# The opening of a decoder layer on one core: a modulation sum ahead of the last diagonal, the shift in two parts, other orders of requests and passes

## The chip, the cores and the metric

The kernel runs on one core of a Trainium2 chip. The metric is device time in microseconds (us) of one execution on that core. The core's engines are called as in the profile: PE is TensorE (matrix products), PEld its weight loads, DVE is VectorE, ACT is ScalarE, POOL is GpSimd, and SP is SyncE, which here only issues transfers. ACT issues transfers too; a letter q behind an engine's name marks its queue of issues.

## The reference

One layer of a hybrid decoder, in float32, for 512 tokens of width 1024. Only its beginning matters here: the modulation of the condition `c`, the first norm, and the first products.

```python
cond = jax.nn.silu(c)
mod = cond @ ada_w[l] + ada_b[l]
sh1, sc1, g1, sh2, sc2, g2 = jnp.split(mod[:, None, :], N_MOD, axis=-1)

u = rms_norm(x, mix_pre_g[l]) * (1.0 + sc1) + sh1
proj = u @ w_in[l]
qk_raw, v, o_pre, gates, glu = jnp.split(
    proj, [2 * D_ML, 3 * D_ML, 4 * D_ML, 4 * D_ML + 2 * H], axis=-1)
...
a, gt = jnp.split(glu, 2, axis=-1)
y = causal_dwconv(a * jax.nn.sigmoid(gt), cv_dw_w[l], cv_dw_b[l])
...
```

`rms_norm` divides each token by the root of its mean square and multiplies by a gain. Behind these lines follow the mLSTM heads, the convolution group, the output projection, and a feed-forward part with a convolution; all of that is the same in both kernels.

## The kernel before, in words

**Layout.** The width of 1024 is cut into 8 blocks of 128 (index k or j), the 512 tokens into 4 tiles of 128 (index tt). `u` is kept with channels on the partitions: u[k] is a block of 128 channels by 512 tokens. Products are made in three terms: every operand z is split into a high part (rounded to the type that TensorE takes, written by ACT) and a low part (z minus the high part, by DVE or POOL). A product is then high by high, high by low and low by high (`mm3`, lines 186 to 190), all added up in one PSUM bank.

**The opening** is what the change touches: lines 118 to 369, run in the first 56 us. It does two things at once. It makes u[0] to u[7], and it makes the first eight output tiles of the gated group (`glu`, banks0, one PSUM bank each), with k as the outer loop: as soon as u[k] and the block of weights for k (`wglu0_k`) are there, its products are added to all eight banks.

- `c` comes as two rows of 512 (`crow`); TensorE spreads them over all partitions (`cps`, line 139) and ACT makes `cb` = silu of that (line 253).
- `x` comes in eight pieces `xn[tt][hf]` of 256 KB, half the width each; the first halves are asked for on SP, the second halves on ACT. For each tile the squares are summed (ACT line 250 for the one half, DVE line 251 for the other), added (`xs`, DVE line 259) and raised to the power -1/2 on POOL (line 260).
- `x_turn` (line 237) multiplies an identity matrix by that factor (`dg`, DVE line 240). With dg as the moving operand TensorE turns blocks 0 to 3 of the tile into `xT_ps` (four banks) with the norm's factor applied (line 242), and with a matrix of ones it makes `rb_ps`, the factor spread over the partitions (line 243). Blocks 4 to 7 come from memory already turned (`xr`, line 328) and use `rb`.
- The modulation of block k is two sums over 1024 products each, `ada` times `cb`, on DVE (`ada_sum`, line 271): one for the scale, one for the shift, into the two columns of `part[k]`. `gsk` holds the gain `gs` (line 331: scale plus 1 plus bias, times the norm's gain; `bp1` and `g32` are small prepared vectors) and the shift `sh` (line 332).
- u[0] high is made by ACT from xT_ps[0] with gs and sh (line 336); DVE makes the exact value xr[0] (line 337) and the low part (line 338). ACT copies the other three banks of xT_ps out (line 286), as TensorE needs the banks for glu.
- `passes` (line 313) issues the 24 products of one k: the pairs (weight high, u high), (weight low, u high), (weight high, u low), each over the banks given. For k=0 it is called for banks 4 to 7 with all three pairs, then for banks 0 to 3. For k of 1 to 3 it is called once over all eight; from k=4 `mm3` is used bank by bank.

**What sets the order.** For SP and TensorE the order of the program text is kept. On DVE, ACT and POOL a scheduler places instructions by a model of their times. The context `opening` (`in_order`, lines 70 to 82) chains all instructions of those three engines that are written inside it, so that they keep the order of the text among themselves; an instruction written elsewhere may still be placed between them. Two of these are lines 398 and 444: `cvw` and `ghalf`, small vectors scaled by 0.5 for the convolution and the head norm, taken from `vec`, whose later columns are asked for at k=1 (line 325).

**Buffers.** `raws` has two buffers of 1 MB for ada, `adas` two of 512 KB for wglu0; a new block is asked for when the one two before has been used. The requests of one k on SP are: wglu0 block k (line 321), ada of block k+1 in two halves (line 225), at k=1 the rest of vec, for k of 1 to 4 one block of xr.

## Time and profile before

| what | value |
|---|---|
| time, three runs | 774.97 us median (774.62 to 776.15) |
| the profiled execution | 774.97 us, of which the span from first to last instruction is 773.2 |
| TensorE busy | 759.2 us, 98% of the span |
| DVE, ACT, POOL busy | 602.0, 399.8 and 350.9 us |
| transferred | 125.33 MB, mean 162 GB/s |

The profile is of one execution. Its timeline rows give the start in us from the span's start, the duration in us, the engine, the line of the kernel, the operation, the tiles it writes and reads, its shape and the count of instructions merged into the row; in brackets stands how long the engine had been idle before it and what ended that. Tile numbers are left out, so that wglu_1h is the high part of the second half of any wglu0 block. Ends of matrix products are modelled, and some of their records are missing.

### The profile page before, as it was taken

Reading aid. Unit: us, or ns where it says so; the run is one execution under the profiler, and the core shown is the slowest. Engines: PE = TensorE matmul, PEld = TensorE weight load, DVE = VectorE, ACT = ScalarE, POOL = GpSimd, SP = SyncE. Lnnn points to the kernel's source line nnn. Section 1 sums busy time; section 2 is a strip of 40 time slices with the busy share of each in tenths; the row PEclk is TensorE's granted clock in tenths of the full one; section 3 lists DMA queues with packets and bytes.
Section 4 is the critical chain, followed back from the end, with each engine's and each line's share of the span. In section 5 each row is a group of like instructions: output and inputs, shape, how many; then the busy total and the mean of one; then the engine's idle time right before and its main releaser. Section 6 shows DMA issues by size and latency. Waiting matters only on the chain.

```text
span 773.2 us, 10567 instructions
## 1 busy us (share of the span) xinstructions
PE 759.2 (98%) x3691; PEld 635.8 (82%) x3691; DVE 602.0 (78%) x955; ACT 399.8 (52%) x753; POOL 350.9 (45%) x286
## 2 busy tenths in 40 slices
PE   7999999999999999999999999999999999999996
PEld 5778898778888888888888998888888888888885
DVE  6977999999999864446858798666555687699996
ACT  5437266687676446472243545444444444455752
POOL 2029677697798644443661456444444440000001
PEclk9999999999999999999999999999999999999998
DMA  9984214204123452434953653332233321777872
GB/s 331 352 309 140 84 55 164 82 29 145 47 81 110 164 169 104 164 108 162 385 183 117 256 193 136 130 129 92 106 117 129 130 90 61 270 269 222 301 260 109
DMA packets 36409, 125.33 MB, mean 162 GB/s; under 512 B 4194, under 2 KB 5634, under 8 KB 30468
## 3 DMA queue, kind: packets, MB, share of 16 engines
q1 hardware_dynamic: 24372, 96.17, 35.4%
q10 hardware_dynamic: 11984, 28.48, 10.6%
q8 instruction: 29, 0.48, 0.2%
q14 instruction: 24, 0.20, 0.1%
HBM read 113.22 MB, written 11.42 MB: 161 GB/s over the span
## 4 chain that ended last, share of the span: by engine, by line
PE 82%; DVE 8%; DMA 5%; ACT 2%; issue 2%; POOL 0%; ACTq 0%; SPq 0%; DVEq 0%; POOLq 0%
PE up L189 10%; PE up L190 10%; PE up L188 10%; PE qko L188 5%; PE qko L189 4%; PE qko L190 4%; PE p L190 3%; PE p L189 3%; PE p L188 3%; PE o L496 2%; PE glu L189 2%; PE glu L190 2%; PE glu L188 2%; DMA wglu<-in_w_glu 2%; PE s L485 2%
## 5 line engine op out<-in xcount | busy, mean ns | idle before, releaser
L694 DVE SCALAR_TENSOR_TENSOR cv<-gt,cvw,cv 128x489 f32<-128x489 f32 (+23 forms) x200 | 136.9, 729 | 2.6 <-ACT cv L682 1.5
L648 POOL TENSOR_TENSOR ro2r<-ro2t,mhalf 128x1 f32<-128x1 f32 x1 | 0.5, 539 | 120.6 <-DVE ro2t L646 120.6
L171 POOL TENSOR_TENSOR wup_1024l<-wup,wup_1024h 128x512 fp32r<-128x512 f32 x20 | 27.8, 1390 | 31.3 <-ACT wup_1024h L170 21.9
L690 POOL TENSOR_TENSOR cs<-cs,cs 128x510 f32<-128x510 f32 (+3 forms) x32 | 41.2, 1289 | 0.2
L171 POOL TENSOR_TENSOR wup_0l<-wup,wup_0h 128x512 fp32r<-128x512 f32 x20 | 27.3, 1367 | 29.4 <-ACT wup_0h L170 29.4
L171 POOL TENSOR_TENSOR wup_1536l<-wup,wup_1536h 128x512 fp32r<-128x512 f32 x20 | 28.1, 1403 | 27.5 <-ACT wup_1536h L170 27.5
L155 DVE SCALAR_TENSOR_TENSOR junk<-ada,cb 128x1024 bf16<-128x1024 f32 x20 | 32.4, 1619 | 7.3 <-DMA ada<-in_adaT 7.1
L189 PE MATMUL up<-u2l,wup_0h 128*128 128x512 f32 (+1 forms) x100 | 36.5, 365 | 0.2 <-DVE u2l L870 0.2
L188 PE MATMUL up<-u2h,wup_0h 128*128 128x512 f32 (+1 forms) x100 | 36.5, 365 | 0.0
L188 PE MATMUL up<-u2h,wup_1024h 128*128 128x512 f32 (+1 forms) x100 | 36.4, 364 | 0.0
L190 PE MATMUL up<-u2h,wup_0l 128*128 128x512 f32 (+1 forms) x100 | 36.4, 364 | 0.0
L188 PE MATMUL up<-u2h,wup_512h 128*128 128x512 f32 (+1 forms) x100 | 36.4, 364 | 0.0
L189 PE MATMUL up<-u2l,wup_512h 128*128 128x512 f32 (+1 forms) x100 | 36.4, 364 | 0.0
L188 PE MATMUL up<-u2h,wup_1536h 128*128 128x512 f32 (+1 forms) x100 | 36.4, 364 | 0.0
L189 PE MATMUL up<-u2l,wup_1536h 128*128 128x512 f32 (+1 forms) x100 | 36.4, 364 | 0.0
L190 PE MATMUL up<-u2h,wup_512l 128*128 128x512 f32 (+1 forms) x100 | 36.4, 364 | 0.0
L190 PE MATMUL up<-u2h,wup_1536l 128*128 128x512 f32 (+1 forms) x100 | 36.4, 364 | 0.0
L190 PE MATMUL up<-u2h,wup_1024l 128*128 128x512 f32 (+1 forms) x100 | 36.4, 364 | 0.0
L189 PE MATMUL up<-u2l,wup_1024h 128*128 128x512 f32 (+1 forms) x100 | 36.3, 363 | 0.0
L171 POOL TENSOR_TENSOR wup_512l<-wup,wup_512h 128x512 fp32r<-128x512 f32 x20 | 27.7, 1384 | 14.8 <-ACT wup_512h L170 14.8
L688 ACT ACTIVATE cs<-gt,cvw 128x511 f32<-128x511 f32 (+4 forms) x40 | 27.4, 715 | 9.5 <-POOL cs L690 4.5
L170 ACT ACTIVATE wup_1024h<-wup 128x512 fp32r<-128x512 f32 x22 | 13.9, 630 | 24.7 <-PE up L189 20.1
(1046 smaller groups left out, 2641.6 us busy)
## 6 DMA issues: line engine op xcount, KB each, us to landing
wup<-in_w_up SPq DMA_DIRECT2D x22, 1024.0 KB, 6.8
wqko<-in_w_qko SPq DMA_DIRECT2D x12, 1024.0 KB, 4.8
ada<-in_adaT ACTq DMA_DIRECT2D x20, 512.0 KB, 4.7
ada<-in_adaT SPq DMA_DIRECT2D x16, 512.0 KB, 6.9
wo<-in_w_out SPq DMA_DIRECT2D x8, 1024.0 KB, 4.8
spare<-in_adaT ACTq DMA_DIRECT2D x12, 512.0 KB, 7.2
wd<-in_w_down SPq DMA_DIRECT2D x6, 768.0 KB, 5.9
g2kept<-g2d SPq DMA_DIRECT2D x11, 384.0 KB, 7.3
```

Of the source, the lines that this page charges most:

```text
L155: t = V.scalar_tensor_tensor(out=junk, in0=r, scalar=1.0, in1=cb, op0=ALU.mult, op1=ALU.mult, accum_out=mod[:, i : i + 1])
L170: S.activation(hi[:, :n], src, AF.Copy)
L171: (eng or G).tensor_tensor(out=lo[:, :n], in0=src, in1=hi[:, :n].bitcast(F32), op=ALU.subtract)
L188: PE.matmul(ps, a[0], b[0], start=start, stop=False)
L189: PE.matmul(ps, a[0], b[1], start=False, stop=False)
L190: PE.matmul(ps, a[1], b[0], start=False, stop=stop)
L485: PE.matmul(sp[:, :n], ks[d][:, cc * P : (cc + 1) * P], qs[d][:, cc * P :], start=d == 0, stop=d == 1)
L496: PE.matmul(o[:, : DH + 2], E[h][cc][:, a : a + P], vs[h][cc], start=cc == 0, stop=cc == tt)
L648: G.tensor_tensor(out=r, in0=t, in1=mhalf[:, :1], op=ALU.pow)
L688: S.activation(t[:, d:], cvx[j][:, : T - d], AF.Copy, scale=w(CK - 1 - d))
L690: G.tensor_tensor(out=side[:, d:], in0=side[:, d:], in1=t[:, d:], op=ALU.add)
L694: last_tap[0] = V.scalar_tensor_tensor(out=cp[:, d:], in0=cvx[j][:, : T - d], scalar=w(CK - 1 - d), in1=cp[:, d:], op0=ALU.mult, op1=ALU.add)
```

## The change

Six edits, all in or around the opening.

1. Requests: on SP, x's first piece is asked for ahead of `c`; `c` and the first columns of `vec` (before: on ACT) follow it, then x's other first halves. The shift half of ada's block 0 is asked for in two pieces of 256 KB.
2. In `x_turn` the rb product is issued ahead of the four xT products.
3. `bp1` and `g32` are made ahead of the loop over x's tiles instead of behind the sums.
4. The scale sum of block 0 stands on DVE ahead of the last tile's `x_turn`. The shift sum of block 0 is made in two halves of 512; the gain is computed between them, the bias is added to the first half's result, and the second half's is added to that.
5. At k=0: xr[0] is made by ACT instead of DVE, the two sums for block 1 stand on DVE between the weight splits and ahead of u[0] low, and the products go in the order: banks 4 to 7 with u high, banks 0 to 3 with u high, then all eight banks with u low.
6. `cvw` and `ghalf` are chained behind the last DVE instruction of the loop.

```diff
@@ -118,13 +118,15 @@
     vec = const.tile([P, NVEC], F32, name="vec")
     cb = const.tile([P, D], F32, name="cb")
     crow = slots.tile([P, T], F32, tag="t", name="crow"), slots.tile([P, T], F32, tag="t", name="crow")
-    for hf in range(2):
-        nc.sync.dma_start(crow[hf][:1, :], c[hf * T : (hf + 1) * T].rearrange("(a n) -> a n", a=1))
     xn = [[slot(f"xn{tt}_{hf}") for hf in range(2)] for tt in range(NT)]
+    FIRST = VEC["mix_pre_g"][1]
     for tt in range(NT):
         for hf in range(2):
             (nc.scalar if hf else nc.sync).dma_start(xn[tt][hf], x[tt * P : (tt + 1) * P, hf * T : (hf + 1) * T])
-    FIRST = VEC["mix_pre_g"][1]
+        if tt == 0:
+            for hf in range(2):
+                nc.sync.dma_start(crow[hf][:1, :], c[hf * T : (hf + 1) * T].rearrange("(a n) -> a n", a=1))
+            nc.sync.dma_start(vec[:, :FIRST], vecs[:, :FIRST])
 
     def vcol(name, i):
         a = VEC[name][0] + i
@@ -221,12 +223,11 @@
     def first_load(k):
 
         r = raws.tile([P, 2048], F32, tag="raw", name=f"ada{k}")
-        for i in range(2):
-            nc.sync.dma_start(r[:, i * D : (i + 1) * D], adaT[k][:, i * D : (i + 1) * D])
+        for a, b in ((0, D), (D, 2 * D)) if k else ((0, D), (D, D + T), (D + T, 2 * D)):
+            nc.sync.dma_start(r[:, a:b], adaT[k][:, a:b])
         first.append(r)
 
     first_load(0)
-    nc.scalar.dma_start(vec[:, :FIRST], vecs[:, :FIRST])
 
     opening = in_order()
     opening.__enter__()
@@ -238,9 +239,23 @@
 
         dg = slot(f"dg{tt}")[:, :P]
         V.tensor_scalar(out=dg, in0=ident, scalar1=xs[:, 1:], scalar2=None, op0=ALU.mult)
+        PE.matmul(rb_ps[:, tt * P : (tt + 1) * P], ones, dg, start=True, stop=True)
         for j in range(TURNED):
             PE.matmul(xT_ps[j][:, tt * P : (tt + 1) * P], xn[tt][j // NT][:, j % NT * P : (j % NT + 1) * P], dg, start=True, stop=True)
-        PE.matmul(rb_ps[:, tt * P : (tt + 1) * P], ones, dg, start=True, stop=True)
+
+    bp1 = const.tile([P, KT], F32, name="bp1")
+    V.tensor_scalar(out=bp1, in0=vcols("ada_b", 0, 2 * KT).rearrange("p (j two) -> p j two", two=2)[:, :, 0], scalar1=1.0, scalar2=None,
+                    op0=ALU.add)
+    g32 = const.tile([P, KT], F32, name="g32")
+    V.tensor_scalar(out=g32, in0=vcols("mix_pre_g", 0, KT), scalar1=RD, scalar2=None, op0=ALU.mult)
+    part = {}
+
+    def ada_sum(k, i):
+        if i == 0:
+            part[k] = small.tile([P, 2], F32, tag="adap", name=f"adap{k}")
+        junk = small.tile([P, D], BF16, tag="junk", bufs=1, name=f"junk{k}_{i}")
+        V.scalar_tensor_tensor(out=junk, in0=first[k][:, i * D : (i + 1) * D], scalar=1.0, in1=cb, op0=ALU.mult, op1=ALU.mult,
+                               accum_out=part[k][:, i : i + 1])
 
     xT_ps = [mmbank(f"xT{j}") for j in range(TURNED)]
     rb_ps = atbank("rb")
@@ -258,28 +273,23 @@
         last = small.tile([P, 2], F32, tag="gsk", name=f"xs{tt}")
         V.tensor_scalar(out=last[:, :1], in0=xsq[:, :1], scalar1=xsq[:, 1:], scalar2=D * EPS, op0=ALU.add, op1=ALU.add)
         G.tensor_tensor(out=last[:, 1:], in0=last[:, :1], in1=mhalf[:, :1], op=ALU.pow)
+    ada_sum(0, 0)
     x_turn(NT - 1, last)
     rb = slot("rb_s")
     S.activation(rb, rb_ps, AF.Copy)
 
-    part = {}
-
-    def ada_sum(k, i):
-        if i == 0:
-            part[k] = small.tile([P, 2], F32, tag="adap", name=f"adap{k}")
-        junk = small.tile([P, D], BF16, tag="junk", bufs=1, name=f"junk{k}_{i}")
-        V.scalar_tensor_tensor(out=junk, in0=first[k][:, i * D : (i + 1) * D], scalar=1.0, in1=cb, op0=ALU.mult, op1=ALU.mult,
-                               accum_out=part[k][:, i : i + 1])
-
-    for i in range(2):
-        ada_sum(0, i)
-
-    bp1 = const.tile([P, KT], F32, name="bp1")
-    V.tensor_scalar(out=bp1, in0=vcols("ada_b", 0, 2 * KT).rearrange("p (j two) -> p j two", two=2)[:, :, 0], scalar1=1.0, scalar2=None,
-                    op0=ALU.add)
-    g32 = const.tile([P, KT], F32, name="g32")
-    V.tensor_scalar(out=g32, in0=vcols("mix_pre_g", 0, KT), scalar1=RD, scalar2=None, op0=ALU.mult)
     xr = [slot(f"xr{j}") for j in range(KT)]
+
+    gsk0 = small.tile([P, 2], F32, tag="gsk", name="gsk0")
+    for a in (D, D + T):
+        junk = small.tile([P, D], BF16, tag="junk", bufs=1, name=f"junk0_{a}")
+        V.scalar_tensor_tensor(out=junk[:, :T], in0=first[0][:, a : a + T], scalar=1.0, in1=cb[:, a - D : a - D + T], op0=ALU.mult,
+                               op1=ALU.mult, accum_out=part[0][:, 1:])
+        if a == D:
+            V.tensor_scalar(out=gsk0[:, :1], in0=part[0][:, :1], scalar1=bp1[:, :1], scalar2=g32[:, :1], op0=ALU.add, op1=ALU.mult)
+            V.tensor_scalar(out=part[0][:, :1], in0=part[0][:, 1:], scalar1=vcol("ada_b", 1), scalar2=None, op0=ALU.add)
+        else:
+            V.tensor_tensor(out=gsk0[:, 1:], in0=part[0][:, 1:], in1=part[0][:, :1], op=ALU.add)
 
     def x_out(j, eng):
         if eng is S:
@@ -310,8 +320,8 @@
 
     banks0 = [mmbank(f"glu{i}") if i < 4 else atbank(f"glu{i}") if i < 6 else cvbank(f"glu{i}") for i in range(G0)]
 
-    def passes(wk, k, which):
-        for a, b in ((0, 0), (1, 0), (0, 1)):
+    def passes(wk, k, which, sides=((0, 0), (1, 0), (0, 1))):
+        for a, b in sides:
             for i in which:
                 PE.matmul(banks0[i], blk(wk, i)[a], u[k][b], start=k == 0 and a == b, stop=False)
 
@@ -326,23 +336,25 @@
         if 1 <= k <= TURNED:
             j = TURNED + k - 1
             nc.sync.dma_start(xr[j], xT[j - TURNED])
-        gsk = small.tile([P, 2], F32, tag="gsk", name=f"gsk{k}")
+        gsk = small.tile([P, 2], F32, tag="gsk", name=f"gsk{k}") if k else gsk0
         gs, sh = gsk[:, :1], gsk[:, 1:]
-        V.tensor_scalar(out=gs, in0=part[k][:, :1], scalar1=bp1[:, k : k + 1], scalar2=g32[:, k : k + 1], op0=ALU.add, op1=ALU.mult)
-        V.tensor_scalar(out=sh, in0=part[k][:, 1:], scalar1=vcol("ada_b", 2 * k + 1), scalar2=None, op0=ALU.add)
+        if k:
+            V.tensor_scalar(out=gs, in0=part[k][:, :1], scalar1=bp1[:, k : k + 1], scalar2=g32[:, k : k + 1], op0=ALU.add, op1=ALU.mult)
+            V.tensor_scalar(out=sh, in0=part[k][:, 1:], scalar1=vcol("ada_b", 2 * k + 1), scalar2=None, op0=ALU.add)
         hi, lo = u[k]
         if k == 0:
             wk[1] = w_split(r[:, T:], "wglu0_0_1", eng=V)
             S.activation(hi, xT_ps[0], AF.Identity, scale=gs, bias=sh)
-            V.tensor_scalar(out=xr[0], in0=xT_ps[0], scalar1=gs, scalar2=sh, op0=ALU.mult, op1=ALU.add)
+            ada_sum(1, 0)
+            wk[0] = w_split(r[:, :T], "wglu0_0_0", eng=V)
+            S.activation(xr[0], xT_ps[0], AF.Identity, scale=gs, bias=sh)
+            ada_sum(1, 1)
             V.tensor_tensor(out=lo, in0=xr[0], in1=hi.bitcast(F32), op=ALU.subtract)
-            wk[0] = w_split(r[:, :T], "wglu0_0_0", eng=V)
             for j in range(1, TURNED):
                 x_out(j, S)
-            for i in range(2):
-                ada_sum(1, i)
-            passes(wk, k, range(4, G0))
-            passes(wk, k, range(4))
+            for which in (range(4, G0), range(4)):
+                passes(wk, k, which, ((0, 0), (1, 0)))
+            passes(wk, k, range(G0), ((0, 1),))
             continue
         if k >= TURNED:
             V.scalar_tensor_tensor(out=xr[k], in0=xr[k], scalar=gs, in1=rb, op0=ALU.mult, op1=ALU.mult)
@@ -358,7 +370,7 @@
         if k < TURNED:
             V.tensor_tensor(out=lo, in0=xr[k], in1=hi.bitcast(F32), op=ALU.subtract)
         else:
-            V.scalar_tensor_tensor(out=lo, in0=xr[k], scalar=sh, in1=hi.bitcast(F32), op0=ALU.add, op1=ALU.subtract)
+            last_u = V.scalar_tensor_tensor(out=lo, in0=xr[k], scalar=sh, in1=hi.bitcast(F32), op0=ALU.add, op1=ALU.subtract)
         if k + 1 < KT:
             ada_sum(k + 1, 1)
         if k < 4:
@@ -370,6 +382,10 @@
     for i, ps in enumerate(banks0):
         glu_ps[i // 2, i % 2] = ps
 
+    def behind_opening(op):
+        tc.add_manual_dep(op.ins, last_u.ins.name, mybir.DependencyInfo(mybir.DependencyClass.NoSync, mybir.DependencyReason.DATA),
+                          reason="order on VectorE")
+
     cvx = [None] * KT
 
     def glu_gate(i):
@@ -395,7 +411,7 @@
         glu_gate(i)
 
     cvw = const.tile([P, CK * KT], F32, name="cvw")
-    V.tensor_scalar(out=cvw, in0=vcols("cv_dw_w", 0, CK * KT), scalar1=0.5, scalar2=None, op0=ALU.mult)
+    behind_opening(V.tensor_scalar(out=cvw, in0=vcols("cv_dw_w", 0, CK * KT), scalar1=0.5, scalar2=None, op0=ALU.mult))
 
 
     vs = [None] * H
@@ -441,7 +457,7 @@
         return t
 
     ghalf = const.tile([P, KT], F32, name="ghalf")
-    V.tensor_scalar(out=ghalf, in0=vcols("ml_norm_g", 0, KT), scalar1=0.5, scalar2=None, op0=ALU.mult)
+    behind_opening(V.tensor_scalar(out=ghalf, in0=vcols("ml_norm_g", 0, KT), scalar1=0.5, scalar2=None, op0=ALU.mult))
     hy = [None] * (2 * KT)
 
     heads = {}
```

## The prediction

> **What bounds the kernel now.** First the page:
>
> ```profile
> span 773.2 us, 10567 instructions
> ...
> PE 759.2 (98%) x3691; PEld 635.8 (82%) x3691; DVE 602.0 (78%) x955; ACT 399.8 (52%) x753; POOL 350.9 (45%) x286
> ```
>
> TensorE lacks 14 us of the span, and the change lies in the first 56 us. So I read the opening's timeline engine by engine (start, duration, engine, line, operation, tiles; in brackets the idle time before and what ended it), TensorE first, for the places where it stood.
>
> ```profile
> 2.38 3.75 PE L139 MATMUL cps<-crow,ones 1*128 1x512 f32 x4 [2.38 <-DMA crow<-in_c]
> ...
> 12.71 1.06 PE L242 MATMUL xT<-dg,xn 128*128 128x128 f32 x8
> 13.60 0.39 PE L243 MATMUL rb<-dg,ones 128*128 128x128 f32 x2
> 15.86 1.19 PE L316 MATMUL glu<-uh,wglu_1h 128*128 128x512 f32 x4 [1.87 <-ACT uh L336]
> ...
> 20.54 1.07 PE L316 MATMUL glu<-ul,wglu_0h 128*128 128x512 f32 x4
> 22.38 1.19 PE L316 MATMUL glu<-uh,wglu_0h 128*128 128x512 f32 x4 [0.77 <-ACT uh L352]
> ...
> 33.40 1.07 PE L316 MATMUL glu<-uh,wglu_0h 128*128 128x512 f32 x4
> ...
> 38.84 0.39 PE L188 MATMUL glu<-uh,wglu_0h 128*128 128x512 f32 x1
> 39.18 0.50 PE L189 MATMUL glu<-ul,wglu_0h 128*128 128x512 f32 x1
> ...
> 55.41 0.39 PE L188 MATMUL glu<-uh,wglu_0h 128*128 128x512 f32 x1
> ```
>
> One k of the loop takes 38.84 - 33.40 = 5.44 us of TensorE, 0.23 a matmul. It stands at 15.86; at 22.38 (the four matmuls from 20.54 occupy 0.91, so it is free at 21.45: 0.93 lost); a little at k=4 (38.84 to 39.18 is 0.34, not 0.23) and at k=7. What it waits for is made on VectorE:
>
> ```profile
> 9.25 0.69 DVE L251 SCALAR_TENSOR_TENSOR xjunk<-xn 128x512 f32<-128x512 f32 x1
> ...
> 10.59 0.21 DVE L259 TENSOR_SCALAR xs<-xsq 128x1 f32<-128x1 f32 x1
> 11.46 0.29 DVE L240 TENSOR_SCALAR dg<-ident,xs 128x128 f32<-128x128 f32 x1 [0.67 <-POOL xs L260]
> 11.66 1.22 DVE L271 SCALAR_TENSOR_TENSOR junk<-ada,cb 128x1024 bf16<-128x1024 f32 x1
> ...
> 12.92 1.22 DVE L271 SCALAR_TENSOR_TENSOR junk<-ada,cb 128x1024 bf16<-128x1024 f32 x1
> ...
> 14.53 0.20 DVE L332 TENSOR_SCALAR gsk<-adap,vec 128x1 f32<-128x1 f32 x1
> ...
> 15.84 0.81 DVE L337 TENSOR_SCALAR xr<-xT,gsk 128x512 f32<-128x512 f32 x1
> ...
> 20.94 0.29 DVE L398 TENSOR_SCALAR cvw<-vec 128x248 f32<-128x248 f32 x1 [0.36 <-DMA vec<-in_vecs]
> ...
> 21.22 0.21 DVE L332 TENSOR_SCALAR gsk<-adap,vec 128x1 f32<-128x1 f32 x1
> ...
> 30.96 0.69 DVE L171 TENSOR_TENSOR wglu_0l<-wglu,wglu_0h 128x512 fp32r<-128x512 f32 x1 [0.73 <-ACT wglu_0h L170]
> ...
> 38.38 0.74 DVE L361 SCALAR_TENSOR_TENSOR ul<-xr,gsk,uh 128x512 fp32r<-128x512 f32 x1
> ...
> 54.54 1.27 DVE L361 SCALAR_TENSOR_TENSOR ul<-xr,gsk,uh 128x512 fp32r<-128x512 f32 x1 [1.84 <-ACT uh L355]
> 59.66 0.69 DVE L379 SCALAR_TENSOR_TENSOR gt<-gt,glu 128x512 f32<-128x512 f32 x1 [3.85 <-ACT gt L377]
> ```
>
> It idles 0.67 before the last diagonal and then does two whole modulation sums before the first shift exists (14.73). At 20.94 two vectors for much later work, waiting for their transfer, stand between k=1's gain and its shift. ul(4) ends at 39.12 and TensorE wants it at 39.07; ul(7) ends at 55.81, wanted at 55.64: there the two are level. A successor starts about 0.09 before its forerunner's row ends (11.46 + 0.29 against 11.66); I count starts. ScalarE, between them:
>
> ```profile
> 7.09 1.00 ACT L253 ACTIVATE cb<-cps 128x1024 f32<-128x1024 f32 x1
> ...
> 14.02 0.60 ACT L263 ACTIVATE rb_s<-rb 128x512 f32<-128x512 f32 x1 [4.16 <-PE rb L243]
> 14.52 0.62 ACT L170 ACTIVATE wglu_1h<-wglu 128x512 fp32r<-128x512 f32 x1
> 15.04 0.77 ACT L336 ACTIVATE uh<-xT,gsk 128x512 fp32r<-128x512 f32 x1
> 15.70 0.63 ACT L170 ACTIVATE wglu_0h<-wglu 128x512 fp32r<-128x512 f32 x1
> 16.22 1.57 ACT L286 ACTIVATE xr<-xT 128x512 f32<-128x512 f32 x3
> ...
> 21.52 0.81 ACT L352 ACTIVATE uh<-xr,gsk 128x512 fp32r<-128x512 f32 x1 [2.69 <-DVE gsk L332]
> ```
>
> **The change, part by part.** *First shift.* The first sum moves into the hole behind xs at 10.59: it starts near 10.72 and costs 12.92 - 11.66 = 1.26, so the last diagonal goes from 11.46 to 11.98. Queued behind it on VectorE are that diagonal and the shift; TensorE waits for the diagonal, but took its matmuls up only at 12.71, from a backlog, and 11.98 + 0.29 is before that. After the diagonal (0.20 to the next start) come a half sum (as long as the square of a half row, 0.69, and 0.04 for the read that follows, as 1.26 is to 1.22), the gain 0.20, first part plus bias 0.13, second half 0.73, final addition 0.20: 2.19, shift at 14.17. The vectors bp1 and g32 leave this chain for the start of VectorE's queue. With the rb matmuls first in each tile, rb is ready at 12.71 + 0.39 = 13.10; ScalarE's copy and wglu_1h (0.52 each, from 14.02, 14.52 and 15.04) end at 14.2. So uh(0) goes from 15.04 to 14.2, TensorE's first loop matmul from 15.86 to 15.02: -0.84.
>
> *k=0.* From uh(0)'s start S VectorE does wglu_1l 0.60, a sum 1.26, wglu_0l 0.60, a sum 1.26, ul 0.60, gain and shift of k=1 0.40: shift at S + 4.7. xr(0) (0.81) is ScalarE's now, and the vectors (0.36 of waiting, 0.28 to the shift's start) are gone. uh(1), 0.81 more, is there at S + 5.5 = 19.7; TensorE is free at 15.02 + 5.59 = 20.6. The 0.93 at 22.38 goes. Two margins are thin. ul(0) comes at S + 4.4: the old order, which asks for it after 8 matmuls (S + 2.8), would have stalled; the new one asks after 16 (S + 4.6). The last copy of xT, pushed back by xr(0), ends at S + 0.66 + 0.52 + 0.66 + 1.57 = S + 3.4, just as TensorE comes to its bank (S + 0.82 + 0.34 + 10 x 0.23 = S + 3.5). I take +0.1 for both; bounds 0 and +0.3.
>
> *Vectors behind the loop.* cvw and ghalf fall after ul(7), into VectorE's 3.85 us of idle before 59.66: nothing, or their 0.28 if that cover went.
>
> *Requests.* On SyncE's queue x's first piece goes ahead of c, and c, the first columns of vec and one more request for ada0 (split in two) are issued among and behind x:
>
> ```profile
> 0.80 0.63 SPq L122 DMA_DIRECT2D crow<-in_c  x2
> 1.48 1.77 SPq L126 DMA_DIRECT2D xn<-in_x  x4
> 5.04 0.80 SPq L225 DMA_DIRECT2D ada<-in_adaT  x2
> ...
> 20.42 0.81 SPq L225 DMA_DIRECT2D ada<-in_adaT  x2
> ...
> 22.00:24.00 2.00, 1.62 (x7) 1.36 (x8) 2.00 (x5) 1.97 (x4) 0.00 (x0) 1.00 0.85 225
> ```
>
> x's first piece is asked for 0.68 earlier; three small requests (0.63 and about 0.4) put SyncE's later pieces some 0.35 later, and ScalarE's lose vec's request ahead of them. c comes later: its 2 KB rows may run after one piece of x or after all of it, so the bounds are 0.4 (the later issue) and 6.8 (VectorE squares x's last piece at 9.25; c started cps at 2.38). Nearest is a wait of one or two pieces; with 1.5 us cps ends at 7.6, cb at 8.6, and through the last two squares, which follow cb on ScalarE, xs(3) comes at 8.6 + 0.7 + 0.87 + 0.2 = 10.4, as now: x's half microsecond is spent there. Taken: 0, bounds -0.5 and +0.6; beyond them begins rival 3. bp1 and g32 wait for vec at the head of VectorE's queue, the squares behind them; x ends that idle time today, so 0, bound +0.5. The request that the cut of ada0 adds costs SyncE 0.4 after x's: 0.
>
> [...]
>
> ```profile
> 4.00:8.00 4.00, 2.73 (x6) 0.94 (x5) 1.93 (x7) 2.26 (x6) 1.38 (x2) 1.00 1.05 403
> 61.00:115.00 54.00, 54.00 (x280) 46.46 (x279) 49.96 (x82) 28.18 (x52) 41.70 (x37) 1.00 0.27 97
> ```
>
> (Columns of these window rows: length, busy time of TensorE, its weight loads, VectorE, ScalarE and GpSimd, granted clock, share of the transfer engines, GB/s.)
>
> *k=4 and k=7.* With VectorE 2 us ahead these waits go: 0.11 and about 0.2.
>
> *Sum.* k=1 on TensorE from 22.38 to 20.6: -1.8; k=4 and k=7 -0.3; thin margins +0.1: -2.0. The profiled execution is the median one, 774.97, of which 1.77 lie around its span. 774.97 - 2.0 = **773.0**. From 61 us on TensorE is busy throughout, as the second row shows for the next 54 us, so a lead there is the kernel's.
>
> **Rivals.** *1. The transfers pace the loop.* At 30.96 VectorE waits for a weight block, and the chain of waits there runs over a transfer:
>
> ```profile
> 22.65 7.62 DMA wglu<-in_w_glu
> ```
>
> If that block lands when it does now but for 0.3 (the earlier start of the stream), ul(4) ends at 38.8, TensorE waits for it at k=4, and 0.3 of the 1.8 remain, with 0.2 at k=7: **774.5**. For it: the request lies 7.62 us in the queue, and the bytes are as many as before. Against it: in 22 to 24 the transfers made 225 GB/s at a share of 0.85, so the queue was not full, and the request for ada3 at 20.42 had waited for VectorE's sum of k=1, which now ends nearly 3 us earlier.
>
> *2. ada0 arrives late for the early sum.* It was asked for at 5.04; that the sum at 11.66 did not wait is all the rows prove. At that end the sum holds the diagonal until 12.92, S is 15.2 and k=1 starts at 21.6: -0.8 for -1.8, **774.0**. The request has no reason to come later than 5.04, and the stream ahead of it is the same x.
>
> *3. Slower: c arrives behind x.* cb stands ahead of two squares on ScalarE; from cb's end to the last diagonal it is a square 0.7, xs to diagonal 0.87, xs(3) 0.2, sum 0.13 + 1.26: 3.2. The gain is gone once S passes 16, the diagonal 13.8, cb's end 10.6, c's second row 7.7. If c comes with x's last piece, at 9.2, cps ends at 12.9, cb at 13.9, S is 19.3 and k=1 starts at 25.7: +3.3, **778.3**. For it: c stands behind x in the same queue now. Against: behind one piece of SyncE's four, not all.
>
> **How the numbers follow.** Forecast 50 in 100, rival 1 25, rival 2 11, rival 3 8, the page's rule 2, and 4 for instructions after the opening that the scheduler may place anew, which I cannot price. 0.2% is 1.55 us, about what a measurement here tells from no change: faster is below 773.4, slower above 776.5. The forecast's own range is 772.4 to 773.9 by its bounds; 43 of its 50 lie under 773.4, and 4 of rival 1's, where the queue paces only in part: faster 0.47. Rival 3 and part of the unpriced: slower 0.11. Same 0.42. The range 772.3 to 775.6 leaves out rival 3, most of the unpriced and the forecast's lower tail.
>
> **What would show it.** Right: first loop matmul near 15.0; no idle before k=1; half sums of 0.69; cvw's row behind ul(7). Rival 1: idle before the ul matmul of k=4, and over 2 us of VectorE's time spent waiting for k=3's weight block. Rival 2: VectorE idle before the first sum, on ada. Rival 3: cps starting past 5 us and the squares waiting behind cb. I am wrong altogether if TensorE is 2 us ahead at 25 us and still at 61 us, and the end does not move.

## The result and the profile after

Before 774.8 us (median of 4), after **780.39** us (median of 4, 779.73 to 781.25): the ratio is 1.0073, with a 95% interval of 1.0056 to 1.009. The kernel became slower by 5.6 us; 773.0 was forecast, and 780.39 lies outside the range of 772.3 to 775.6. The profiled execution took 780.38 us. Its page:

```profile
span 778.7 us, 10571 instructions
...
PE 761.6 (98%) x3691; PEld 637.1 (82%) x3691; DVE 605.4 (78%) x957; ACT 400.4 (51%) x754; POOL 351.0 (45%) x286
```

TensorE lacks 17.1 us of the span, 3.1 more than before, and is busy 2.4 us longer with the same products. So part of the loss is waiting and part is slower work. The timeline of TensorE in the changed kernel says where:

```profile
4.27 3.75 PE L141 MATMUL cps<-crow,ones 1*128 1x512 f32 x4 [4.27 <-DMA crow<-in_c]
...
14.90 0.49 PE L242 MATMUL rb<-dg,ones 128*128 128x128 f32 x2 [0.60 <-DVE dg L241]
...
17.75 1.20 PE L326 MATMUL glu<-uh,wglu_1h 128*128 128x512 f32 x4 [1.46 <-ACT uh L347]
...
40.37 0.50 PE L191 MATMUL glu<-ul,wglu_0h 128*128 128x512 f32 x1 [0.17 <-DVE ul L373]
...
210.29 1.48 PE L501 MATMUL s<-q_0c,k_2c 128*128 128x512 f32 x2 [2.01 <-DVE so L536]
211.56 1.91 PE L501 MATMUL s<-q_1c,k_3c 128*128 128x512 f32 x2
```

There are two places. In the opening the first loop matmul starts at 17.75 where it started at 15.86: +1.89. The wait ahead of k=1 is gone as forecast, which gives some of that back; k=4's product with u low stands 1.19 later than before (40.37 against 39.18). Then nothing happens for 170 us, until TensorE stands still for 2.01 us at 210, which it did not do before, waits for `so` (the output gate of head 0 times its turned result), and goes on with products that take 1.9 us a pair. The matching pair of before, aligned by order, starts 3.25 us earlier than 210.29, and behind the slow pairs the difference is 5.05. From there to the end it stays between 5 and 6.5.

**The opening.** VectorE in the changed kernel:

```profile
5.56 0.17 DVE L247 TENSOR_SCALAR bp<-vec 128x8 f32<-128x8 f32 x1 [3.60 <-DMA vec<-in_vecs]
...
9.59 0.69 DVE L266 SCALAR_TENSOR_TENSOR xjunk<-xn 128x512 f32<-128x512 f32 x1 [1.41 <-DMA xn<-in_x]
...
11.97 0.69 DVE L266 SCALAR_TENSOR_TENSOR xjunk<-xn 128x512 f32<-128x512 f32 x1 [1.35 <-DMA xn<-in_x]
...
12.90 1.22 DVE L257 SCALAR_TENSOR_TENSOR junk<-ada,cb 128x1024 bf16<-128x1024 f32 x1
...
14.56 0.29 DVE L241 TENSOR_SCALAR dg<-ident,xs 128x128 f32<-128x128 f32 x1 [0.43 <-POOL xs L275]
14.77 0.69 DVE L286 SCALAR_TENSOR_TENSOR junk<-ada,cb 128x512 bf16<-128x512 f32 x1
...
16.66 0.16 DVE L292 TENSOR_TENSOR gsk<-adap 128x1 f32<-128x1 f32 x1
```

The last square of x, at 9.25 before, waits for its piece until 11.97. The half sums cost 0.69 each, and the last addition, which makes the shift, starts 2.10 behind the diagonal (16.66 to 14.56; the forecast's terms give 1.99). So the chain is nearly as forecast, but all of it is late because of x: the diagonal by 2.6 us (11.98 forecast), the first loop matmul by 2.7 (15.02). The chain of waits shows why x is late (start, duration, what):

```profile
0.80 3.28 DMA xn<-in_x
...
4.10 0.34 ACTq L125
...
4.47 7.47 DMA xn<-in_x
...
11.97 0.70 DVE xjunk L266 x2
```

ScalarE's queue asked for a late piece of x only at 4.10, just behind the landing of x's first piece, and for the last one at 4.47; before, the last piece was asked for at 3.00. Eight requests had gone out ahead of the one at 4.10 (the two pieces of x's first tile, c's two rows, vec, and three more pieces): the ninth went out only when the first had landed (at 4.08). Behind that gap in the requests, from 6 to 8 us, the transfers ran dry (share 0.70). Two windows of after, then the same two of before:

```profile
4.00:6.00 2.00, 1.73 (x2) 0.83 (x3) 0.44 (x3) 0.72 (x2) 0.00 (x0) 1.00 1.04 339
6.00:8.00 2.00, 2.00 (x3) 0.33 (x1) 1.45 (x7) 0.72 (x2) 0.92 (x1) 1.00 0.70 201
```

```profile
4.00:6.00 2.00, 2.00 (x3) 0.33 (x1) 0.90 (x4) 0.72 (x2) 0.00 (x0) 1.00 1.06 407
6.00:8.00 2.00, 0.73 (x4) 0.61 (x4) 1.03 (x5) 1.54 (x4) 1.38 (x2) 1.00 1.05 399
```

From 6 to 8 us 201 GB/s came in where 399 did: 0.4 MB less, and another 0.14 MB from 4 to 6, two of x's 256 KB pieces.

**Behind the opening.** The scheduler placed the instructions of VectorE, ScalarE and GpSimd anew there. VectorE of after, then of before, ahead of `so` of head 0:

```profile
196.46 4.26 DVE L528 TENSOR_SCALAR hn<-hn,fac 128x256 f32<-128x256 f32 x4
200.64 1.37 DVE L710 SCALAR_TENSOR_TENSOR cv<-gt,cvw,cv 128x504 f32<-128x504 f32 x2
...
202.53 7.11 DVE L710 SCALAR_TENSOR_TENSOR cv<-gt,cvw,cv 128x503 f32<-128x503 f32 x11
209.56 0.68 DVE L536 SCALAR_TENSOR_TENSOR so<-so,hT 128x512 f32<-128x512 f32 x1
```

```profile
202.07 1.13 DVE L512 TENSOR_SCALAR hn<-hn,fac 128x256 f32<-128x256 f32 x4
203.12 2.63 DVE L694 SCALAR_TENSOR_TENSOR cv<-gt,cvw,cv 128x497 f32<-128x497 f32 x4
205.66 0.67 DVE L520 SCALAR_TENSOR_TENSOR so<-so,hT 128x512 f32<-128x512 f32 x1
```

hn (the head's result times a factor) stands earlier in the new order, with thirteen convolution taps between it and `so` where there were four, and its four instructions take 4.26 us for 1.13. GpSimd in after says with what they met:

```profile
196.57 1.39 POOL L173 TENSOR_TENSOR wqko_0l<-wqko,wqko_0h 128x512 fp32r<-128x512 f32 x1
197.92 1.34 POOL L706 TENSOR_TENSOR cs<-cs,cs 128x509 f32<-128x509 f32 x1
199.22 1.35 POOL L728 TENSOR_TENSOR ysq<-ysq,ydl 128x512 f32<-128x512 f32 x1
```

hn's first instruction starts 0.11 us ahead of the first of these three rows and takes 0.35. The other three start at 196.73, 198.03 and 199.33, 0.11 to 0.16 behind one row each, take 1.38 to 1.39 and end 0.15 behind that row's end. Before, GpSimd was idle from 201.99 to 205.67, and hn fell into that, at 0.34 each. GpSimd's next row of before shows the idle time:

```profile
205.67 1.31 POOL L171 TENSOR_TENSOR wqko_1024l<-wqko,wqko_1024h 128x512 fp32r<-128x512 f32 x1 [3.68 <-PE v L189]
```

The taps (0.64 from start to start) show no such loss: all 200 of them take 0.69 to 0.75, beside GpSimd and alone.

### The profile page after: what moved, and what is told of

Same layout as the page of the kernel before. It is cut to its first block, busy times and chain, and to the rows that moved or that the text cites. A ratio compares the mean times of both kernels' runs of the same rounds, so it can differ in the third digit from the quotient of the medians.

```text
span 778.7 us, 10571 instructions
## 1 busy us (share of the span) xinstructions
PE 761.6 (98%) x3691; PEld 637.1 (82%) x3691; DVE 605.4 (78%) x957; ACT 400.4 (51%) x754; POOL 351.0 (45%) x286
## 4 chain that ended last, share of the span: by engine, by line
PE 70%; DVE 19%; DMA 4%; ACT 3%; issue 2%; POOL 1%; ACTq 0%; DVEq 0%; SPq 0%; POOLq 0%
PE up L191 10%; PE up L192 10%; PE up L190 10%; DVE cv L710 9%; PE p L1161 4%; PE glu L191 3%; PE glu L192 3%; PE glu L190 3%; PE mixa L190 2%; PE mixa L192 2%; PE mixa L191 2%; PE mixb L191 2%; PE mixb L190 2%; PE mixb L192 2%; PE p L191 2%
## 5 line engine op out<-in xcount | busy, mean ns | idle before, releaser
L710 DVE SCALAR_TENSOR_TENSOR cv<-gt,cvw,cv 128x502 f32<-128x502 f32 (+24 forms) x200 | 137.3, 728 | 2.6 <-ACT cv L698 1.4
```

The lines of the kernel that those rows point to most:

```text
L710: last_tap[0] = V.scalar_tensor_tensor(out=cp[:, d:], in0=cvx[j][:, : T - d], scalar=w(CK - 1 - d), in1=cp[:, d:], op0=ALU.mult, op1=ALU.add)
```

## The experiments

In twelve of the fourteen kernels the order behind the opening is held fast, so that a change in the opening cannot move it: a list of positions for each of the three engines, taken from the kernel before ("old order") or from the changed one ("new order"), is chained like this, and nothing else is touched:

```diff
+    traced = nc.cur_bb.bb.instructions
+    a = next(i for i in reversed(range(len(traced))) if traced[i] is opened) + 1
+    for eng, places in ((V.engine, ORDER_V), (S.engine, ORDER_S), (G.engine, ORDER_G)):
+        mine = [ins for ins in traced[a:] if ins.engine == eng]
+        for p, n in zip(places, places[1:]):
+            tc.add_manual_dep(mine[n], mine[p].name, mybir.DependencyInfo(mybir.DependencyClass.NoSync, mybir.DependencyReason.DATA),
+                              reason="given order")
```

The lists hold only what is written behind the opening. An instruction that is written there but has its operands early, as cvw and ghalf have in the kernel before, can still be placed among the opening's own instructions, so this place is the scheduler's in these kernels too; it matters in experiments 6 and 7.

The ratios are to the kernel before, run beside them; 0.1% is 0.77 us.

| kernel | us | ratio (95%) |
|---|---|---|
| changed kernel | 780.39 | 1.0073 (1.0056 to 1.009) |
| after_o_before: its opening, old order | 774.84 | 1.0009 (0.9998 to 1.0021) |
| before_o_after: old opening, new order | 780.56 | 1.0075 (1.0051 to 1.0098) |
| after_o_after_hn: hn with two tensors | 780.5 | 1.0081 (1.0059 to 1.0102) |
| after_o_after_stt: hn as two-step form | 782.07 | 1.0112 (1.0096 to 1.0127) |
| after_o_after_so: `so` sooner | 781.22 | 1.0094 (1.0078 to 1.0109) |
| after_o_after_hnact: hn on ScalarE | 774.49 | 0.9998 (0.9984 to 1.0012) |
| after_nobehind: cvw, ghalf free | 775.64 | 1.0026 (1.0017 to 1.0035) |
| before_reqnew_o_before: only the requests | 776.74 | 1.0041 (1.0024 to 1.0058) |
| after_veclast_o_before | 774.66 | 1.0000 (0.9987 to 1.0013) |
| after_reqold: all but the requests | 773.4 | 0.9984 (0.9968 to 1.0) |
| after_reqold_o_before: same, old order | 772.8 | 0.9984 (0.9972 to 0.9996) |
| before_k0_o_before: only k=0, vectors | 773.0 | 0.9977 (0.9968 to 0.9986) |
| before_shift_o_before: only first shift | 773.73 | 0.9988 (0.9977 to 0.9999) |
| after_reqold_o_before_hnact | **771.69** | 0.9960 (0.9947 to 0.9974) |

**1. Opening or order?** after_o_before and before_o_after; the edit of both is the chain above.

> The changed kernel with its whole opening; only the order in which VectorE, ScalarE and GpSimd issue their instructions behind the opening is fixed to the order they have in the kernel before. Theory A (two causes: the opening is late, +1.2 us that TensorE still shows at 140 us, and the newly placed instructions behind it cost the other 4.2 us at 207 to 214 us and at 268 us): hn's four VectorE instructions return from 4.26 to about 1.2 us, the wait of 2.01 us at 210 us goes, and the time is 776.0 us (775.3 to 776.8). Theory B (the late opening by itself makes the later waits; the order behind it is only how they show): the waits at 210 us and 268 us stay in some form and the time is 779 to 781. Theory C (the later order is all of it and the opening's lateness is made good further on): 774.3 to 775.2.

> The kernel before with its own opening; only the order of VectorE, ScalarE and GpSimd behind the opening is fixed to that of the changed kernel. Theory A: hn runs beside the GpSimd instructions and `so` comes late, so that TensorE waits near 209 us: 777.5 to 779.5 us, with the first loop matmul at 15.9 us as before. If the collision of hn with GpSimd is a matter of a microsecond's alignment it may come out smaller, 775.5 to 777.5, but above 775.2. Theory B: with the opening in time nothing is late, 774.5 to 775.2 us.

The changed opening with the old order costs 0.09%, at most 0.21%; the old opening with the new order costs 0.75%. So the order behind the opening is nearly all of the loss, whatever the opening does. after_o_before fell into theory C's range in microseconds; against the kernel before beside it (773.99 us) it is 0.7 us slower by the ratio, but the interval reaches down to nothing. This is the opening's balance, gains and costs together: experiments 6 and 7 take it apart. before_o_after came out above what A had for it: A had given the opening too large a share.

**2. Is it hn's form?** after_o_after_hn and after_o_after_stt:

```diff
-            V.tensor_scalar(out=hv, in0=hv, scalar1=fac[:, tt : tt + 1], scalar2=None, op0=ALU.mult)
+            V.tensor_tensor(out=hv, in0=hv, in1=fac[:, tt : tt + 1].to_broadcast([P, DH]), op=ALU.mult)
```

> The changed kernel with its own order behind the opening held fast, and one edit: hn is multiplied by a VectorE instruction with two tensor operands, the second one the factor's column broadcast, in place of the one with a scalar operand. The same numbers are computed. Theory A with the scalar form waiting for GpSimd (three of the four took 1.38 us each and ended with a GpSimd instruction): the four take 0.35 to 0.5 us each, hn is done some 2.5 us sooner, the wait at 210 us goes or shrinks below 0.5 us, and the time is 776.5 to 777.5 us. Rival (the order of the convolution taps ahead of `so` is what makes it late, hn's form is no matter): 779.5 to 781 us.

```diff
-            V.tensor_scalar(out=hv, in0=hv, scalar1=fac[:, tt : tt + 1], scalar2=None, op0=ALU.mult)
+            V.scalar_tensor_tensor(out=hv, in0=hv, scalar=fac[:, tt : tt + 1], in1=ones[:, :1].to_broadcast([P, DH]), op0=ALU.mult, op1=ALU.mult)
```

> The changed kernel with its own order behind the opening held fast, and one edit: hn is multiplied by the two-step VectorE instruction (SCALAR_TENSOR_TENSOR, factor's column, then times a column of ones), the form that the convolution taps have, which took 0.72 us for about 500 elements beside GpSimd and alone alike. The same numbers are computed. Theory D (the instructions of hn wait for GpSimd's because of their form, and that is what makes `so` late): the four take 0.3 to 0.45 us each, 1.5 us together in place of 4.26, everything on VectorE behind them comes 2.7 us sooner, `so` starts near 206.9 us, TensorE's 2.01 us at 210 us and the half-rate matmuls behind it (1.6 us) go, and the time is 776.3 to 777.3 us. Rival E (VectorE's place in the order alone makes `so` late): hn's form changes nothing, 779.5 to 781 us.

Both missed. The row of hn in the first, then in the second:

```profile
195.78 4.75 DVE L598 TENSOR_TENSOR hn<-hn,fac 128x256 f32<-128x256 f32 x4
```

```profile
197.96 4.78 DVE L598 SCALAR_TENSOR_TENSOR hn<-hn,fac,ones 128x256 f32<-128x256 f32 x4
```

All three forms take longer beside GpSimd: one hn there takes 1.38 us as it was and 1.50 to 1.52 in these two forms. So these runs took nothing away and could not tell the theories apart; that 780.5 lies in the range of the rival says no more. What sets the taps apart is not their form: in the second run hn has it too. Their running sum lies in PSUM, while hn's operands all lie in SBUF, but that this is the cause was not shown (the last section goes on with this).

**3. Is it the place of `so`?** after_o_after_so moves four entries of the new order's list for VectorE (`so` of head 0 from behind 11 taps to behind 4, and of head 1 ahead of one modulation sum). The lines stand for the list of positions, in words:

```diff
-ORDER_V: hn0 x4, 2 taps, Md1, 11 taps, so0, tap, so0 ... sum 16, sum 17, ydl7, sum 18, so1, so1
+ORDER_V: hn0 x4, 2 taps, Md1, 4 taps, so0, tap, so0 ... sum 16, sum 17, ydl7, so1, so1, sum 18
```

> The changed kernel with its own order behind the opening held fast but for four instructions: the two of `so` of head 0 stand behind four convolution taps in place of eleven (hT, their input, is done at 205.4 us), and the two of head 1 stand ahead of the modulation sum that waited 2.0 us for its transfer at 265 us. hn keeps its form and its place beside GpSimd. Rival E: `so` at about 205.5 us, the 2.01 us at 210 us, the matmuls at half rate behind it and the 1.23 us at 268 us go: 775.3 to 776.5 us. Theory D alone (what counts is the 2.7 us of VectorE's time that hn loses): the time lost turns up at the next thing that waits for VectorE, and 778 us or more stay.

`so` did start at 205.49 and the wait at 210 us went, with the slow products behind it: at 214 us TensorE was 3.3 us ahead of the changed kernel. But the time stayed, 781.22, as theory D had it. TensorE lost the lead again at the next `so`. Where VectorE stands by then is seen at the first of the later modulation sums (for the gates and the second half of the layer). The row of before, of after, and of this kernel:

```profile
252.78 1.22 DVE L155 SCALAR_TENSOR_TENSOR junk<-ada,cb 128x1024 bf16<-128x1024 f32 x1
```

```profile
259.11 1.22 DVE L157 SCALAR_TENSOR_TENSOR junk<-ada,cb 128x1024 bf16<-128x1024 f32 x1
...
265.19 1.70 DVE L157 SCALAR_TENSOR_TENSOR junk<-ada,cb 128x1024 bf16<-128x1024 f32 x1 [2.01 <-DMA ada<-in_adaT]
...
266.82 1.27 DVE L536 SCALAR_TENSOR_TENSOR so<-so,hT 128x512 f32<-128x512 f32 x2
```

```profile
260.44 1.22 DVE L226 SCALAR_TENSOR_TENSOR junk<-ada,cb 128x1024 bf16<-128x1024 f32 x1
```

VectorE is 6.3 us late in the changed kernel and 7.7 here. What stands on it between 59.7 us and this sum is the same set of instructions in before and after; counted from start to next start they take 184.9 us before and 189.3 after, and hn has 3.4 of the 4.4 more; the rest of the 6.3 is idle time of VectorE. Windows of before and of after from 140 to 255 us show that VectorE has no room for that:

```profile
140.00:255.00 115.00, 115.00 (x581) 96.41 (x580) 112.00 (x181) 81.53 (x165) 90.34 (x75) 1.00 0.22 77
```

```profile
140.00:255.00 115.00, 112.55 (x542) 92.48 (x543) 111.93 (x177) 77.13 (x156) 90.68 (x75) 0.99 0.23 81
```

TensorE is busy for all 115 us before, and VectorE for 112. There are two bounds here, not one. So moving `so` only moved the wait, and a third theory, F, was formed.

**4. Is it VectorE's time?** after_o_after_hnact keeps the new order and gives hn to ScalarE:

```diff
-            V.tensor_scalar(out=hv, in0=hv, scalar1=fac[:, tt : tt + 1], scalar2=None, op0=ALU.mult)
+            on_act.append(S.activation(hv, hv, AF.Copy, scale=fac[:, tt : tt + 1]).ins)
```

> The changed kernel with its own order behind the opening held fast, but hn's sixteen instructions are taken from VectorE and done by ScalarE, which has time to spare (66% busy from 190 to 215 us). The same numbers are computed. Theory F (VectorE is the second bound from 140 to 255 us, where it is busy 99% of the time as TensorE is; its instructions are the same in number up to the first modulation sum behind 250 us, and the 4.4 us that they take longer there, 3.4 of them hn beside GpSimd, are what makes `so` of head 0 and of head 1 late): the first of those sums starts at 252 to 254 us in place of 259.1, no wait above 0.6 us at 210 and at 268 us, and the time is 774 to 775.5 us, as with the order of the kernel before. Rival (the order itself, whatever VectorE's time): 778 us or more.

It came as theory F had it: 5.9 us below the changed kernel, with the same opening and the same order.

```profile
204.93 0.67 DVE L607 SCALAR_TENSOR_TENSOR so<-so,hT 128x512 f32<-128x512 f32 x1
...
252.98 1.22 DVE L226 SCALAR_TENSOR_TENSOR junk<-ada,cb 128x1024 bf16<-128x1024 f32 x1
...
260.97 1.27 DVE L607 SCALAR_TENSOR_TENSOR so<-so,hT 128x512 f32<-128x512 f32 x2
```

The sum of 259.11 starts at 252.98, `so` of head 1 at 260.97 for 266.82, and TensorE waits at neither. The edit takes hn's own 2.9 us (what it costs VectorE up to there in the kernel before) off VectorE along with the 3.4 of waiting, 6.3 in all. So it shows that VectorE's time is the bound: the same order, with less work on VectorE, loses nothing. That hn's waiting makes up most of the extra work is read from the trace; that it alone is the whole cause is not shown, since no run takes the waiting away and leaves hn where it is.

**5. What called up the new order?** after_nobehind and after_reqold each undo one edit and leave the order to the scheduler:

```diff
-    behind_opening(V.tensor_scalar(out=cvw, in0=vcols("cv_dw_w", 0, CK * KT), scalar1=0.5, scalar2=None, op0=ALU.mult))
+    V.tensor_scalar(out=cvw, in0=vcols("cv_dw_w", 0, CK * KT), scalar1=0.5, scalar2=None, op0=ALU.mult)
```

> The changed kernel with one edit undone: the two vectors' factors (cvw, ghalf) are not held behind the loop; nothing fixes the order behind the opening, and the scheduler places hn and `so` of head 0 nearly as in the kernel before (157 taps ahead of hn, 2 between hn and `so`; the changed kernel has 145 and 13, the kernel before 156 and 4). If the placement is what costs (theory A): 774.5 to 776.0 us, no wait of TensorE near 210 us. If the later loss came from the opening's lateness or from something else in the change: 779 to 781 us.

```diff
+    for hf in range(2):
+        nc.sync.dma_start(crow[hf][:1, :], c[hf * T : (hf + 1) * T].rearrange("(a n) -> a n", a=1))
     xn = [[slot(f"xn{tt}_{hf}") for hf in range(2)] for tt in range(NT)]
...
-        if tt == 0:
-            for hf in range(2):
-                nc.sync.dma_start(crow[hf][:1, :], c[hf * T : (hf + 1) * T].rearrange("(a n) -> a n", a=1))
-            nc.sync.dma_start(vec[:, :FIRST], vecs[:, :FIRST])
...
     first_load(0)
+    nc.scalar.dma_start(vec[:, :FIRST], vecs[:, :FIRST])
```

> The changed kernel with one part undone: the requests for x, c and the vectors are as in the kernel before. Nothing fixes the order behind the opening; the scheduler places 157 taps ahead of hn and 2 between hn and `so` (changed kernel 145 and 13). If the requests cost about 2 us by themselves and, by way of the scheduler, the bad order too: 772.4 to 774.0 us, 6 to 8 us below the changed kernel. If another of its edits still brings a costly order: 775 us or more.

Undoing either is enough to lose the bad order: 775.64 and 773.4, both as expected, and no wait of TensorE near 210 us in either. after_nobehind is still slower than the kernel before by 0.26% (0.17 to 0.35): it keeps the new requests. So neither of the two makes the bad order by itself; it comes out of the scheduler's model when they stand together with the rest, and what it costs can't be read from the diff.

**6. What do the requests cost?** before_reqnew_o_before puts only the new requests of experiment 5's diff into the kernel before; after_veclast_o_before takes vec's request back:

> The kernel before with only the new requests for x, c and the vectors (x's first piece ahead of c, c and the vectors behind it), its order behind the opening held fast. If the requests alone make x late (theory A): last square of x near 11.8 us in place of 9.25, first loop matmul near 18 us in place of 15.9, the wait at 22 us stays, and the time is 2.0 to 2.6 us above that of the kernel before, 776.3 to 777.4 us. Rival (the requests cost nothing by themselves, and the early sum or the vectors at the head of VectorE's queue make the opening late): 774.2 to 775.2 us.

```diff
-            nc.sync.dma_start(vec[:, :FIRST], vecs[:, :FIRST])
...
     first_load(0)
+    nc.scalar.dma_start(vec[:, :FIRST], vecs[:, :FIRST])
```

> The changed kernel with its order behind the opening as in the kernel before, and the request for the vectors put behind x again; x's first piece stays ahead of c. Theory G (the last pieces of x are asked for only once the first requests have landed, eight being under way at most, so that every request put ahead of x's tail delays one more piece): two pieces of x in place of three are asked for after 4 us, the last square of x starts at 10.3 to 11.3 us (9.25 before, 11.7 with all new requests), and the time is 773.2 to 774.5 us. Rival (c behind x's first piece is what counts, through cb's place ahead of two squares): last square at 11.7 us as now, 774.5 to 775.2 us.

The requests alone cost 0.41% (0.24 to 0.58), with the first loop matmul at 17.82 as expected. Part of this is not x's lateness. In this kernel cvw still stands between k=1's gain and shift, and waits there for the rest of vec:

```profile
24.20 0.29 DVE L469 TENSOR_SCALAR cvw<-vec 128x248 f32<-128x248 f32 x1 [1.67 <-DMA vec<-in_vecs]
```

In the kernel before that wait was 0.36. TensorE waits 2.10 us ahead of k=1 here, and is 1.95 us late at the first loop matmul but 3.3 at k=1. The changed kernel has cvw elsewhere and doesn't pay this. In the other pair, after_o_before against after_reqold_o_before, they cost 0.25%, 1.9 us. With vec taken back the last square starts at 11.12 us, 0.57 sooner than in after_o_before, as theory G has it; but three pieces of x, not two, were asked for late (3.58, 3.77 and 4.25 us), since ScalarE's queue sent vec's request first of all. The time, 774.66 us, lies in the range of the rival and can't be told from after_o_before's. So the place of the square speaks for theory G, and the time does not decide.

**7. What is left of the forecast gain?** after_reqold_o_before is the changed kernel with the requests of the kernel before (the diff of experiment 5) and the old order:

> The changed kernel with the requests for x, c and the vectors as in the kernel before, and with the order behind the opening as in the kernel before; the sum ahead of the last diagonal, the shift in parts, the new place of the vectors' factors and the other pass order stay. Theory A: the last square of x is done near 9.3 us as before, the first loop matmul starts at 14.9 to 15.3 us, no wait at 22 us, and the time is 772.7 to 773.6 us. Rival (the early sum or the two-part shift delays the last diagonal whatever the requests): the first loop matmul at 15.9 us or later and 774.5 us or more.

The time is as expected, 772.8 us and -0.16% (-0.28 to -0.04), 1.2 us, and there is no wait at 22 us. The first loop matmul starts at 15.45 us, not at 14.9 to 15.3. So the two terms were measured apart:

```diff
+            ada_sum(1, 0)
+            wk[0] = w_split(r[:, :T], "wglu0_0_0", eng=V)
+            S.activation(xr[0], xT_ps[0], AF.Identity, scale=gs, bias=sh)
+            ada_sum(1, 1)
...
+            for which in (range(4, G0), range(4)):
+                passes(wk, k, which, ((0, 0), (1, 0)))
+            passes(wk, k, range(G0), ((0, 1),))
```

> The kernel before with only the new order inside k=0 (xr(0) on ScalarE, a modulation sum ahead of each of two VectorE steps, the other pass order) and the two vectors' factors held behind the loop; requests, first shift and the order behind the opening are those of the kernel before. If the k=0 step of the forecast is right (its 0.93 us ahead of k=1 are worth themselves): no wait of TensorE between 15.9 and 38 us, and 0.8 to 1.4 us below the kernel before. Rival (the lead is spent further on, at the transfers of k=3 or k=4): less than 0.4 us.

```diff
+    ada_sum(0, 0)
     x_turn(NT - 1, last)
...
+    for a in (D, D + T):
+        V.scalar_tensor_tensor(out=junk[:, :T], in0=first[0][:, a : a + T], scalar=1.0, in1=cb[:, a - D : a - D + T], op0=ALU.mult,
+                               op1=ALU.mult, accum_out=part[0][:, 1:])
```

> The kernel before with only the new way to the first shift (a modulation sum ahead of the last diagonal, the shift summed in two parts, ada0 in three pieces, rb's matmuls first in each tile, bp1 and g32 ahead); requests, k=0 and the order behind the opening are those of the kernel before. As forecast: uh(0) near 14.2 and the first loop matmul near 15.0 us, 0.84 us below the kernel before. Rival H (ScalarE's copy of rb and wglu_1h, which wait for TensorE's backlog of half-rate matmuls, set uh(0) all the same): first loop matmul at 15.4 us or later, less than 0.4 us gained, and the wait at 22 us as long as before or longer.

k=0 brings -0.23% (-0.32 to -0.14), 1.8 us, above the 0.8 to 1.4 expected, and TensorE's wait at 22 us is gone. (This kernel also has the edit of cvw and ghalf.) Where the time comes from is less plain: in its profiled execution the granted clock falls to 0.61 behind a wait at 15 us, and k=1 starts no earlier than before, at 22.72 for 22.38:

```profile
22.72 1.07 PE L385 MATMUL glu<-uh,wglu_0h 128*128 128x512 f32 x4
```

TensorE leads there by 0.43 us at 61 us and by 1.87 at the end. So the wait is gone and the kernel is faster, but that the one makes the whole of the other is not shown. The first shift alone brings -0.12% (-0.23 to -0.01), 0.9 us, but not where it was expected. VectorE, ScalarE and TensorE of before_shift_o_before:

```profile
11.12 1.23 DVE L325 SCALAR_TENSOR_TENSOR junk<-ada,cb 128x1024 bf16<-128x1024 f32 x1 [0.45 <-DMA ada<-in_adaT]
...
14.37 0.16 DVE L360 TENSOR_TENSOR gsk<-adap 128x1 f32<-128x1 f32 x1
```

```profile
13.88 0.60 ACT L347 ACTIVATE rb_s<-rb 128x512 f32<-128x512 f32 x1 [4.19 <-PE rb L310]
14.38 0.62 ACT L239 ACTIVATE wglu_1h<-wglu 128x512 fp32r<-128x512 f32 x1
14.90 0.77 ACT L415 ACTIVATE uh<-xT,gsk 128x512 fp32r<-128x512 f32 x1
```

```profile
9.81 1.92 PE L312 MATMUL xT<-dg,xn 128*128 128x128 f32 x8
...
13.46 0.39 PE L310 MATMUL rb<-dg,ones 128*128 128x128 f32 x2
...
15.72 1.20 PE L394 MATMUL glu<-uh,wglu_1h 128*128 128x512 f32 x4 [0.98 <-ACT uh L415]
```

The shift is there at 14.5, 0.2 earlier than before, but ScalarE copies rb only at 13.88, because TensorE's turning products still take 1.92 us for eight (1.06 later on) and the last rb is made at 13.46. uh(0) then follows two ScalarE instructions behind. This is rival H, and it leaves the first loop matmul 0.14 us earlier (15.72 for 15.86). The larger gain shows at k=1, which starts at 21.52 for 22.38, but most of it is not the edit's. In the kernel before, cvw and ghalf stand between k=1's gain and shift (the prediction's rows at 20.94 and 21.22), and here the scheduler has put them behind it:

```profile
20.36 0.20 DVE L411 TENSOR_SCALAR gsk<-adap,vec 128x1 f32<-128x1 f32 x1
...
21.08 0.28 DVE L482 TENSOR_SCALAR cvw<-vec 128x248 f32<-128x248 f32 x1
```

From gain to shift it is 0.19 us here and 0.91 before: 0.72 of the 0.86. So the kernel gains 0.9 us (0.1 to 1.8), but how much of that is the shift's in two parts is not shown; its own trace shows 0.14.

**8. The best of it.** after_reqold_o_before_hnact joins after_reqold_o_before with the hn edit of experiment 4:

> The best kernel so far (changed kernel, old requests, old order behind the opening) with hn on ScalarE in place of VectorE. The same numbers are computed. Theory F: TensorE already waits for nothing but 0.28 us at 268 us there, so VectorE's 3 us less work buys at most that: 772.2 to 773.0 us. Rival (VectorE holds TensorE up in ways that the waits of matmuls do not show): 771.5 us or less.

It is faster than both kernels: 771.69 us, -0.40% (-0.53 to -0.26), and below what theory F gave, though not as low as its rival had it (771.5 or less). The wait of 0.28 us at 268 is gone. The spans of the two profiled executions differ by 0.6 us (770.4 and 769.8), the medians by 1.1, and the intervals just overlap; whether more than the 0.6 is real, and where it would come from, stays open.

## Why the prediction was wrong

**The step that failed most** is the last one of its sum: "From 61 us on TensorE is busy throughout, as the second row shows for the next 54 us, so a lead there is the kernel's." TensorE was busy throughout, in that order of instructions, and with the order held fast the step did hold: in after_reqold_o_before TensorE leads the kernel before by 1.72 us at 61 us and by 2.95 at the end of the profiled execution. In the changed kernel the order was another. VectorE was busy for 112 of 115 us beside it, and it was the scheduler that laid out who met whom. The prediction named this, "instructions after the opening that the scheduler may place anew, which I cannot price", and gave it 4 in 100. It cost 5 us (1.0073 for 1.0009). A price could have been had from the trace of before: there one hn took 1.10 us and seven 0.34, and hl from 0.74 to 1.78, so, by an estimate from these rows, each of some dozens of VectorE instructions could lose about a microsecond by meeting GpSimd, on an engine with 3 us to spare.

**Requests** were taken at 0, bounds -0.5 and +0.6; they cost 1.9 us (experiment 6, and +0.41% alone). The working looked for c's lateness, through cb and the squares. c did come late, at 4.27 for 2.38, and cb at 8.05; but that was not what held the squares: x's last pieces were, asked for 1.5 us later because more requests stood ahead of them, and the last of them then took 7.47 us to land. That a ninth request waits for a landing fits three kernels (4.10 us in the changed one, 3.58 in after_veclast_o_before, 2.62 before), but no run changes that alone, and why the last piece took so long is not shown. Rival 3 had the place (the requests) and the sign, with another mechanism; the row that was to show it, cps past 5 us, did not. The bound of +0.5 for bp1 and g32 waiting for vec at the head of VectorE's queue was too small for what happened (the first square at 5.71 for 4.36), but x's tail covered it.

**First shift**, -0.84: the half sums (0.69) came as worked out, the 2.1 us from diagonal to the last addition nearly (1.99), and the early sum started at 11.05 and 11.12 with the old requests (10.72). uh(0) did not come at 14.2 even with the old requests, but at 14.63 and 14.90. The wrong number is "rb is ready at 13.10": in before_shift_o_before the last of it starts at 13.46 and the copy at 13.88, since TensorE was still slow. So the first loop matmul gained 0.14 in before_shift_o_before and 0.41 in after_reqold_o_before, for the 0.84. The 0.9 us that before_shift_o_before gains in time do not confirm the term: most of what its trace gains by k=1 is cvw's new place.

**k=0**, -0.93 and what follows: the mechanism was right. The wait ahead of k=1 is gone in the changed kernel and in every other kernel with this edit. With the vectors behind the loop, but without the other edits, it is worth 1.8 us (1.1 to 2.5), more than forecast; the profiled execution does not show all of that as a lead from k=1, so how far the size was right stays open. The thin margins held; at k=4 0.17 of waiting was left in the changed kernel, and no more than 0.09 with the old requests.

**Vectors behind the loop**: cvw took 1.38 us and ghalf 1.26 there, not 0.28 together, both beside GpSimd. They fell into idle time, so the price of nothing held in the opening; but without this edit the order behind came out harmless.

**The sum**: with the old requests and the old order the other edits give 1.2 us (0.3 to 2.2) for the forecast 2.0: right in kind, and the forecast lies within the interval. The sign of being wrong altogether, a lead at 61 us and an end that does not move, did not come once the order was held fast. Rival 1 (transfers pace the loop) did not show: no wait at k=3 or k=4 in after_reqold_o_before. Rival 2 was there at about a quarter of its price (the last diagonal at 12.20 and 12.27, for 11.98 forecast and 12.92 by the rival): the early sum waited 0.41 and 0.45 us for ada0 with the old requests, and not at all in the changed kernel, where x was later still. The rule to which the chances give 2 in 100 is shown by no run. What the runs show of cutting ada0 in pieces is that the second half sum waited for no transfer, neither at 15.93 in the changed kernel nor at 13.56 in after_reqold_o_before, where x was in time.
